# The last gate columns of four SwiGLU layers, moved behind the first seven products of the down projection

## The chip, the cores and the metric

The kernel runs on one core of one Trainium2 chip. The metric is the device time of one execution in microseconds (us). Before the change three runs gave 892.24, 891.83 and 892.64 us, a median of 892.24 us. A separate execution was profiled: 891.0 us, of which 889.1 us are the span from the first to the last instruction. The core's engines are called as in the profile: PE (matrix products; PEld loads their stationary operand), DVE (vector), ACT (scalar), POOL (general purpose) and SP, which here only issues DMA transfers. Each engine works through its own queue in order.

## The reference, cut to what matters

```
def swiglu_ffn(h, w1, w3, w2):
    return (jax.nn.silu(h @ w1) * (h @ w3)) @ w2
...
for i in range(2):
    h = h + 0.5 * swiglu_ffn(rmsnorm(h, ffn_norm1[i]), ffn1_w1[i], ffn1_w3[i], ffn1_w2[i])
    m = rmsnorm(h, mix_norm[i])
    h = h + (conv_module(m, ...) if i == 0 else mla(m, positions, ...))
    h = h + 0.5 * swiglu_ffn(rmsnorm(h, ffn_norm2[i]), ffn2_w1[i], ffn2_w3[i], ffn2_w2[i])
return rmsnorm(h, final_norm)
```

There are 256 rows (tokens) of 1024 channels in float32; the hidden width of an FFN is 2816. So the program is FFN, convolution, FFN, FFN, attention, FFN. The four FFNs are counted as first to fourth here; the change is in all four and nowhere else.

## The kernel before

*Precision.* Each float32 operand x is split into a high part (cast to the fp32r type, on ACT, line 248 or 216) and a low part (x minus the high part, on DVE, line 249 or 202). A product is three matmuls, low weights by high rows, high by high and high by low (`mm3`, lines 332 to 338). The stationary operand is a tile of 128 rows by 128 channels, the moving one 512 columns of a weight block.

*Weight blocks.* Weights come in blocks of 1 MB (`raw`, 128 x 2048 values, four buffers), are split into `hi` and `lo` (five buffers each, in two halves each) and used in the order of the list `blocks`. `load_ahead` keeps a few blocks loaded and cast ahead of the one in use. `n_used` counts the blocks that the products have taken, and `casts[n, i]` is the pair of instructions (ACT, DVE) that splits half `i` of block `n`. All loads are issued by SP.

*One FFN* (`ffn_in`, line 871). Six chunks of hidden columns, c = 0 to 5, the first five of 512 columns and the last of 256. The up products of a chunk fill PSUM banks `u[m, tb]`: m = 0 is the gate side (w1), m = 1 the other (w3), tb = 0 and 1 are the two halves of 128 rows. In the last chunk (`both`) one bank per tb holds both sides. ACT takes Silu of the gate side, DVE multiplies by the other (lines 1005 to 1011); the result `s` is then turned, because the down projection needs hidden columns on the partitions: DVE transposes blocks of 32 x 32 (line 505, `gt`), four DMAs write it to DRAM (line 509, `gd`), one reads it back rearranged (line 514, `gb`), and ACT and DVE split it into `Gh` and `Gl` (line 890, for the last columns 881). That is a `turn`; there is one for each chunk and tb, and one for both halves of the last chunk (`turn_last`). PSUM has eight banks: four under tag A, three under B, one under C.

*The down projection.* `Gh` and `Gl` hold 22 tiles of 128 hidden columns. Blocks 0 to 3 of w2 (tiles 0 to 7) are not multiplied one by one: seven products of sums (a Strassen-like scheme, `seven_products`, line 374) replace eight. Each is 12 matmuls. It forms sums of the weight blocks on DVE (lines 206 to 212) and sums of the rows, whose splits are the `forms`. The first form, of the sum `z22`, is prepared ahead in `down()`; the other three follow in `forms_of` (lines 367 and 370). The four result banks `o` come from tag A, in the order (0,0), (1,0), (1,1), (0,1); the tile `kept` (p5) holds a copy of the second product until two additions have used it. Then the remaining blocks 4 to 10 (tiles 8 to 21) follow, block by block in `Rows.block` (24 matmuls each), the last two or, in the second and third FFN (`apart`), the last three together bank by bank in `Rows.finish`. Tiles 16 to 19 belong to the fifth chunk (blocks 8 and 9), tiles 20 and 21 to the last chunk (block 10). The first bank that `finish` fills in the second and third FFN takes the first row half through blocks 8, 9 and 10, then the second bank does; the second row half comes third and fourth.

*Order.* A scheduler that simulates the program fixes the order of each engine's queue, mostly by the order in which the source emits the instructions and by when they can start in its simulation. `order(ins, first)` adds an edge: `ins` comes behind `first`. Before the change the Silus and products of the last chunk are emitted ahead of the group of seven products, the turn of the fifth chunk's second half too, and only `turn_last` behind it, with its transposition behind the DVE split of the second half of the next block (block 4) and the last four gates' splits behind the first half of block 5.

Of the kernel before, what the change touches and what calls it, by code (L numbers as in the profile page):

```python
# [11 lines left out]
F32 = mybir.dt.float32  # L12
# [7 lines left out]
P = 128  # L20
# [69 lines left out]
def trunk(ctx: ExitStack, tc: tile.TileContext, x, xt, first, pos, invf, gfin, wdw,  # L90
# [14 lines left out]
    def uid(s):  # L105
        n_uid[0] += 1
        return f"{s}_{n_uid[0]}"
# [4 lines left out]
    def bank(tag, name):  # L112
        return ps.tile([P, 512], F32, tag=tag, name=uid(name), bufs=BANKS[tag])
# [244 lines left out]
    def forms_of(sums, sh, sl, late={}):  # L358
        sh, sl = (z.rearrange("p k t -> p (k t)").rearrange("p (n c) -> p n c", c=512) for z in (sh, sl))
        out = {}  # L360
        for i, (n, x) in enumerate(sums):
            if len(x.shape) == 2:
                high, low = (z[:, i].rearrange("p (t i q) -> p t i q", t=4, q=32) for z in (sh, sl))
                x = x.rearrange("p (i t q) -> p t i q", i=4, q=32)
            else:
                high, low = (z[:, i].rearrange("p (k t) -> p k t", t=P) for z in (sh, sl))
            cast = nc.scalar.copy(high, x)
            if n in late:
                late[n] = cast
            nc.vector.tensor_sub(low, x, high.bitcast(F32))  # L370
            out[n] = [z[:, i].rearrange("p (k t) -> p k t", t=P) for z in (sh, sl)]
        return out

    def seven_products(xh, xl, forms, banks, late={}, ahead=False):


        def rows(a, tb):
            k = slice(4 * a, 4 * a + 4)
            return xh[:, k, tbs(tb)], xl[:, k, tbs(tb)]

        def product(a, b, fresh):
            load_ahead(W_BUFS - 1)
            (hi, lo), = weights(1, False)
            for k in range(4):
                c = slice(k * 512, k * 512 + 512)
                before[:] = [mm3(b, a[0][:, k], a[1][:, k], hi[:, c], lo[:, c], fresh and k == 0, k == 3, before, True)]

        n0 = n_used[0]
        before = []
        c11, c21, c12, c22 = banks[0, 0], banks[1, 0], banks[0, 1], banks[1, 1]  # L390
        def copy(to, b, block):
# [12 lines left out]
        product(forms[0], c22, True)  # L404
        kept = tmp.tile([P, 512], F32, tag="s", name=uid("p5"))
        copy(kept, c22, n0 + 5)
        product(forms[1], c21, False)
        add = urgent(nc.vector.tensor_add)(c12, c21, kept)
        if ahead:
            load_to(n0 + 7)  # L410
        for i in range(PIECES if ahead else 1):
            order(casts[n0 + 5, i][1], add.ins)
        if ahead:
            order(casts[n0 + 4, PIECES - 1][1], add.ins)
        for high, low in gates[-2 * NT:-NT] if not late else ():
            order(low, thirds[n0 + 2].ins)
        late_gates = []
        for high, low in gates[-NT:] if not late else ():
            late_gates.append((high, low))
        product(rows(1, 0), c11, False)  # L420
        product(forms[2], c21, False)
        add = urgent(nc.vector.tensor_add)(c22, c21, kept)
        if ahead:
            load_to(n0 + 8)
        for i in range(PIECES if ahead else 1):
            order(casts[n0 + (7 if ahead else 6), i][1], add.ins)
        if ahead:
# [354 lines left out]
    class Rows:  # L782
# [3 lines left out]
                                                      ((0, 0), (0, 1), (1, 0), (1, 1)))}  # L786
            self.seeded = seeded

        def seven(self, forms, late):
            seven_products(self.zh, self.zl, forms, self.o, late)  # L790

        def mm(self, part, i, tb, d, o, f0, f1, o0=0, o1=512, after=(), after_last=()):
            hi, lo = part
# [75 lines left out]
            return ffn_in(act, X, make_next, beside, apart, SEVEN_UP.get(n, ()), n in SEVEN_DOWN)  # L869

    def ffn_in(act, X, make_next, beside, apart, seven_up, seven_down):
        down_sums, first_form = [], {}
        Gh = act.tile([P, NF, S], F32R, tag="Gh", name=uid("Gh"))
        Gl = act.tile([P, NF, S], F32R, tag="Gl", name=uid("Gl"))
        def turn_last(g):

            bv = turn_blocks(act, g, 4, "g", ())
            order(last_turn[0], casts[n_used[0], PIECES - 1][1].ins)
            gh = Gh[:, NF - 2:, :].rearrange("p f (t i q) -> p (f t) i q", i=4, q=32)
            low = Gl[:, NF - 2:, :].rearrange("p f (t i q) -> p (f t) i q", i=4, q=32)  # L880
            gates.append((nc.scalar.copy(gh, bv), nc.vector.tensor_sub(low, bv, gh.bitcast(F32))))

        def turn(c, tb, w, g):

            n = w // P
            f = slice(4 * c, 4 * c + n)
            bv = turn_blocks(act, g[:, :w], n, "g", (), rows4[:, 2 * c + tb, :] if seven_down and c < 2 else None)
            gh = Gh[:, f, tbs(tb)].rearrange("p t (i q) -> p t i q", q=32)
            low = Gl[:, f, tbs(tb)].rearrange("p t (i q) -> p t i q", q=32)
            gates.append((nc.scalar.copy(gh, bv), nc.vector.tensor_sub(low, bv, gh.bitcast(F32))))  # L890
# [37 lines left out]
        for c in range(6):  # L928
# [18 lines left out]
            for m in range(0 if u else 1 if both else 2):  # L947
# [2 lines left out]
                if X.whole and c == 0 and m == 0:  # L950
                    load_to(4)
                for tb in range(NT):
                    u[m, tb] = bank("A", "u")
                steps = [(k, tb) for k in range(KT) for tb in range(NT)]
                if not (X.whole and c == 0 and m == 0):
                    steps.sort(key=lambda t: (t[0] // kn, t[1]))
# [36 lines left out]
                        load_ahead()  # L993
                if c > 0:
                    beside()
            if both:
                last_s = tmp.tile([P, 512], F32, tag="s", name=uid("s"))
            for tb in range(NT):
                if both:
                    s = last_s.rearrange("p (f t c) -> p t f c", t=NT, c=P)[:, tb]  # L1000
                    ug, uu = (u[0, tb][:, v].rearrange("p (f c) -> p f c", c=P) for v in (slice(w), slice(w, 2 * w)))
                else:
                    s = tmp.tile([P, 512], F32, tag="s", name=uid("s"))
                    ug, uu = u[0, tb], u[1, tb]
                silu = nc.scalar.activation(s, ug, AF.Silu, scale=X.r[tb])  # L1005
                if both and seven_down and tb == 0:
                    load_to(n_used[0] + 3)
                    for i in range(PIECES):
                        order(casts[n_used[0] + 2, i][0], silu.ins)
                mul = urgent(nc.vector.tensor_mul) if c in seven_up or c + 1 in seven_up else nc.vector.tensor_mul  # L1010
                mul(s, s, uu)
                if not both:
                    turn(c, tb, w, s)
        o = Rows(Gh, Gl, NF, make_next is Final, seven_down)
        if seven_down:
            both = (xp.tile([P, KT, S], F32R, tag=tag, name=uid("rows")) for tag in ("Xh", "Xl"))
            late = {2: None, 3: None}
            o.seven({**first_form, **forms_of(down_sums[1:], *both, late)}, late)
            turn_last(last_s)
            for gate in gates[-NT - 2:]:  # L1020
                for ins, cast in zip(gate, casts[n_used[0] + 1, 0]):
                    order(ins, cast.ins)
        stage.append("down")
        for i in range(4 if seven_down else 0, NF // 2 - (3 if apart else 2)):
# [879 lines left out]
```

## Time and profile before

| what | value |
| --- | --- |
| median of three runs | 892.24 us |
| profiled execution, total | 891.0 us |
| its span | 889.1 us |
| mean granted clock of the matrix engine | 0.999 |
| DVE 32 x 32 transpositions of gates (L505, 128x512) | 44, median 707 ns |
| DVE gate products (L1011) | 24 of 128x512, 8 of 128x256 |
| down group of the four FFNs, first matmul | 122.3, 388.8, 562.8, 825.7 us |
| turns issued by SP: writes `gd<-gt`, reads `gb<-gd` and `rows<-gd` | 176 of 64 KB, 28 and 16 of 256 KB |

How to read it: a line of the timeline gives start and duration in us, the engine, the line of the kernel, the operation, the tile written and the tiles read, the shape and a count of merged instructions; in brackets stands how long the engine had been idle and what released it. A line of the list of waits gives the engine and operation that waited, what it waited for, the total in us, how often, and the longest. `L` is a line of the kernel. SPq is SP's queue of DMA issues; its duration is that of the issue, not of the transfer. The matrix engine's ends are modelled, so consecutive matmuls overlap in the listing; starts are used for distances.

### The profile page before, as it was taken

How to read it: one execution, taken by the hardware profiler on the slowest of the kernel's cores; microseconds unless marked ns; L12 is line 12 of the kernel's file. 1: busy time of each engine (PE TensorE's matmuls, PEld its weight loads, DVE VectorE, ACT ScalarE, POOL GpSimd, SP SyncE). 2: the span in 40 equal slices, each digit the busy share in tenths (PEclk: the TensorE clock that was granted, in tenths of full speed). 3: DMA queues.
4: the chain of work that ended last, by engine and by line, in shares of the span. 5: the costliest groups of instructions: out<-in, count | busy, mean ns of one | idle time of the engine just before them, and what ended most of it. 6: DMA issues, size and time to landing. Idle time of an engine off the chain costs nothing.

```text
span 889.1 us, 12241 instructions
## 1 busy us (share of the span) xinstructions
PE 881.5 (99%) x4209; PEld 741.9 (83%) x4209; DVE 768.7 (86%) x1106; ACT 580.2 (65%) x1001; POOL 104.8 (12%) x227
## 2 busy tenths in 40 slices
PE   9999999999999999999999999999999999999997
PEld 7888887898988888888888888888899888888886
DVE  6899999789999899989598999995778679999873
ACT  7667858789887656647385465673777666563762
POOL 1000000079952000000010000001400010000000
PEclk9999999999999999999999999999999999999999
DMA  9884929834216945929859278396644558387451
GB/s 336 302 312 148 390 84 354 330 137 148 96 60 230 328 188 204 360 83 358 293 191 335 93 259 308 116 394 200 224 144 142 190 171 334 99 324 257 160 218 48
DMA packets 68174, 198.94 MB, mean 224 GB/s; under 512 B 7952, under 2 KB 38544, under 8 KB 48784
## 3 DMA queue, kind: packets, MB, share of 16 engines
q1 hardware_dynamic: 67680, 197.47, 62.4%
q8 instruction: 33, 0.54, 0.2%
q10 hardware_dynamic: 432, 0.69, 0.2%
q14 instruction: 29, 0.24, 0.1%
HBM read 181.87 MB, written 16.25 MB: 223 GB/s over the span
## 4 chain that ended last, share of the span: by engine, by line
PE 97%; DVE 1%; ACT 0%; DMA 0%; issue 0%; ACTq 0%
PE u L338 17%; PE u L334 17%; PE u L337 17%; PE o L334 9%; PE o L338 9%; PE o L337 9%; PE u L1060 3%; PE gate L1060 3%; PE o L1296 3%; PE u L438 2%; PE sc L1657 1%; PE tp L473 1%; DVE lo L202 1%; PE pairs L1103 1%; PE a L337 1%; PE a L338 1%
## 5 line engine op out<-in xcount | busy, mean ns | idle before, releaser
L249 DVE TENSOR_TENSOR lo<-raw,hi 128x1024 fp32r<-128x1024 f32 (+1 forms) x228 | 267.0, 1212 | 25.8 <-ACT hi L248 25.2
L248 ACT CAST hi<-raw 128x1024 fp32r<-128x1024 f32 (+1 forms) x230 | 229.1, 1044 | 83.9 <-DMA raw<-in_f2w 31.5
L338 PE MATMUL u<-hi,Xl 128*128 128x512 f32 x592 | 230.4, 389 | 0.0
L337 PE MATMUL u<-hi,Xh 128*128 128x512 f32 x592 | 230.3, 389 | 0.0
L334 PE MATMUL u<-lo,Xh 128*128 128x512 f32 x592 | 229.8, 389 | 0.0
L216 ACT CAST hi<-raw 128x1024 fp32r<-128x1024 f32 x112 | 111.5, 1050 | 59.7 <-DVE raw L202 44.8
L202 DVE TENSOR_TENSOR lo<-raw,hi 128x1024 fp32r<-128x1024 f32 x112 | 132.1, 1216 | 2.5 <-ACT hi L216 2.4
L338 PEld LDWEIGHTS u<-hi,Xl 128*128 128x128 f32 x592 | 111.1, 188 | 23.5 <-DVE Xl L492 0.5
L337 PEld LDWEIGHTS u<-hi,Xh 128*128 128x128 f32 x592 | 111.1, 188 | 23.1
L334 PEld LDWEIGHTS u<-lo,Xh 128*128 128x128 f32 x592 | 111.1, 188 | 23.0
L337 PE MATMUL o<-hi,Gh 128*128 128x512 f32 (+1 forms) x276 | 106.5, 386 | 0.0
L338 PE MATMUL o<-hi,Gl 128*128 128x512 f32 (+1 forms) x276 | 106.5, 386 | 0.0
L334 PE MATMUL o<-lo,Gh 128*128 128x512 f32 (+1 forms) x276 | 106.2, 387 | 0.0
L464 POOL TENSOR_TENSOR ms<-ss 128x1 f32<-128x1 f32 x16 | 8.1, 510 | 592.6 <-ACT junk L456 592.6
L202 DVE TENSOR_TENSOR raw<-raw,raw 128x2048 f32<-128x2048 f32 x32 | 73.2, 2288 | 2.4 <-DMA raw<-in_f1w 1.2
L334 PEld LDWEIGHTS o<-lo,Gh 128*128 128x128 f32 x276 | 51.8, 188 | 10.7 <-DVE lo L202 0.2
L337 PEld LDWEIGHTS o<-hi,Gh 128*128 128x128 f32 x276 | 51.8, 188 | 10.4
L338 PEld LDWEIGHTS o<-hi,Gl 128*128 128x128 f32 x276 | 51.8, 188 | 10.4
L1005 ACT ACTIVATE s<-u,R 128x512 f32<-128x512 f32 (+1 forms) x48 | 30.6, 647 | 36.3 <-PE u L338 35.4
L1149 DVE SCALAR_TENSOR_TENSOR acc<-V,dw,acc 128x128 f32<-128x128 f32 (+1 forms) x174 | 53.9, 392 | 0.0
L1170 ACT ACTIVATE prod<-V,dw 128x128 f32<-128x128 f32 (+1 forms) x128 | 45.6, 415 | 1.8 <-POOL Y L1171 1.0
L826 DVE SCALAR_TENSOR_TENSOR h<-o,rh,h 128x512 f32<-128x512 f32 (+1 forms) x18 | 13.0, 720 | 27.2 <-PE o L338 27.2
(271 smaller groups left out, 1303.8 us busy)
## 6 DMA issues: line engine op xcount, KB each, us to landing
raw<-in_f2w SPq DMA_DIRECT2D x66, 1024.0 KB, 6.0
raw<-in_f1w SPq DMA_DIRECT2D x62, 1024.0 KB, 7.0
raw<-in_cw SPq DMA_DIRECT2D x12, 1024.0 KB, 6.2
gd<-gt SPq DMA_DIRECT2D x176, 64.0 KB, 3.8
gb<-gd SPq DMA_DIRECT2D x28, 256.0 KB, 3.3
rows<-gd SPq DMA_DIRECT2D x16, 256.0 KB, 3.0
raw<-in_wo SPq DMA_DIRECT2D x4, 1024.0 KB, 4.8
hd<-rows SPq DMA_DIRECT2D x56, 64.0 KB, 2.3
```

Source lines behind the costliest of these rows:

```text
L202: ins = nc.vector.tensor_sub(out, left, right)
L216: casts[n, i] = nc.scalar.copy(hi[:, c], raw[:, c]), sub(lo[:, c], raw[:, c], hi[:, c].bitcast(F32))
L248: casts[len(loaded), i] = (nc.scalar.copy(hi[:, c], raw[:, c]), low.tensor_sub(lo[:, c], raw[:, c], hi[:, c].bitcast(F32)))
L249: low.tensor_sub(lo[:, c], raw[:, c], hi[:, c].bitcast(F32)))
L334: mm = nc.tensor.matmul(o, ah, bl, start=start, stop=False, skip_group_check=seeded)
L337: nc.tensor.matmul(o, ah, bh, start=False, stop=False, skip_group_check=seeded)
L338: return nc.tensor.matmul(o, al, bh, start=False, stop=stop, skip_group_check=seeded)
L1005: silu = nc.scalar.activation(s, ug, AF.Silu, scale=X.r[tb])
L1060: mm = nc.tensor.matmul(u[:, t], w[:, c], X.x[:, k, t], start=(k == 0), stop=(k == KT - 1))
L1149: dve_last.append(nc.vector.scalar_tensor_tensor(out if j == j1 - 1 else y, v, w, y, op0=ALU.mult, op1=ALU.add))
L1170: prods_last.append(nc.scalar.activation(p, v, AF.Copy, scale=w))
L1296: p = nc.tensor.matmul(o[tb, d], (Zl if kind == "x" else Zh)[:, f, tbs(tb)], (lo if kind == "l" else hi)[:, c], start=(f, kind) == (0, "l" ...
```

## The change

Five things, in all four FFNs:

1. The last chunk's products go to banks of tag B in place of A, so that the four result banks of the group are those of the fifth chunk.
2. The Silus and products of the last chunk are emitted behind the group of seven products, each behind the split (ACT or DVE) of the second half of block 5.
3. The turn of the fifth chunk's second half (c = 4, tb = 1) is emitted behind the group too (`late_turns`), its transposition behind the DVE split of the second half of block 4. `turn_last` has no edge of its own any more.
4. The copy `kept` goes into the place of the sum z22 (`down_sums[0][1]`), whose split has been made, in place of a temporary tile, since both temporary tiles stay in use longer.
5. The splits of the last four gates: the first two stay behind the first half of block 5, the third goes behind the first half of block 6, the last behind the second half of block 6. The edge that held a weight cast behind the last chunk's first Silu is gone.

```diff
-    def seven_products(xh, xl, forms, banks, late={}, ahead=False):
+    def seven_products(xh, xl, forms, banks, late={}, ahead=False, kept=None):
...
-        kept = tmp.tile([P, 512], F32, tag="s", name=uid("p5"))
+        if kept is None:
+            kept = tmp.tile([P, 512], F32, tag="s", name=uid("p5"))
...
             bv = turn_blocks(act, g, 4, "g", ())
-            order(last_turn[0], casts[n_used[0], PIECES - 1][1].ins)
...
-                    u[m, tb] = bank("A", "u")
+                    u[m, tb] = bank("B" if both else "A", "u")
...
-            if both:
-                last_s = tmp.tile([P, 512], F32, tag="s", name=uid("s"))
-            for tb in range(NT):
-                if both:
-                    s = last_s.rearrange("p (f t c) -> p t f c", t=NT, c=P)[:, tb]
-                    ug, uu = (u[0, tb][:, v].rearrange("p (f c) -> p f c", c=P) for v in (slice(w), slice(w, 2 * w)))
+            for tb in range(0 if both else NT):
+                s = tmp.tile([P, 512], F32, tag="s", name=uid("s"))
+                nc.scalar.activation(s, u[0, tb], AF.Silu, scale=X.r[tb])
+                mul = urgent(nc.vector.tensor_mul) if c in seven_up or c + 1 in seven_up else nc.vector.tensor_mul
+                mul(s, s, u[1, tb])
+                if 2 * c + tb < 9:
+                    turn(c, tb, w, s)
                 else:
...
-                silu = nc.scalar.activation(s, ug, AF.Silu, scale=X.r[tb])
-                if both and seven_down and tb == 0:
-                    load_to(n_used[0] + 3)
-                    for i in range(PIECES):
-                        order(casts[n_used[0] + 2, i][0], silu.ins)
...
+                    late_turns.append((c, tb, w, s))
...
-            o.seven({**first_form, **forms_of(down_sums[1:], *both, late)}, late)
+            o.seven({**first_form, **forms_of(down_sums[1:], *both, late)}, late, down_sums[0][1])
+
+            for t in late_turns:
+                turn(*t)
+                order(last_turn[0], casts[n_used[0], PIECES - 1][1].ins)
+            last_s = tmp.tile([P, 512], F32, tag="s", name=uid("s"))
+            for tb in range(NT):
+                s = last_s.rearrange("p (f t c) -> p t f c", t=NT, c=P)[:, tb]
+                ug, uu = (u[0, tb][:, v].rearrange("p (f c) -> p f c", c=P) for v in (slice(w), slice(w, 2 * w)))
+                silu = nc.scalar.activation(s, ug, AF.Silu, scale=X.r[tb])
+                mul = nc.vector.tensor_mul(s, s, uu)
+                for ins, cast in zip((silu, mul), casts[n_used[0] + 1, PIECES - 1]):
+                    order(ins, cast.ins)
             turn_last(last_s)
-            for gate in gates[-NT - 2:]:
-                for ins, cast in zip(gate, casts[n_used[0] + 1, 0]):
+            for gate, behind_, i in zip(gates[-4:], (1, 1, 2, 2), (0, 0, 0, PIECES - 1)):
+                for ins, cast in zip(gate, casts[n_used[0] + behind_, i]):
                     order(ins, cast.ins)
```

More of the change, by code (lines that the diff above doesn't have):

```diff
@@ L787, in __init__, with seven @@
             self.seeded = seeded
-        def seven(self, forms, late):
-            seven_products(self.zh, self.zl, forms, self.o, late)
+        def seven(self, forms, late, kept):
+            seven_products(self.zh, self.zl, forms, self.o, late, kept=kept)
         def mm(self, part, i, tb, d, o, f0, f1, o0=0, o1=512, after=(), after_last=()):
@@ L871, in ffn_in @@
     def ffn_in(act, X, make_next, beside, apart, seven_up, seven_down):
-        down_sums, first_form = [], {}
+        down_sums, first_form, late_turns = [], {}, []
         Gh = act.tile([P, NF, S], F32R, tag="Gh", name=uid("Gh"))
@@ L995, in ffn_in @@
                     beside()
-            if both:
-                last_s = tmp.tile([P, 512], F32, tag="s", name=uid("s"))
-            for tb in range(NT):
-                if both:
-                    s = last_s.rearrange("p (f t c) -> p t f c", t=NT, c=P)[:, tb]
-                    ug, uu = (u[0, tb][:, v].rearrange("p (f c) -> p f c", c=P) for v in (slice(w), slice(w, 2 * w)))
-                else:
-                    s = tmp.tile([P, 512], F32, tag="s", name=uid("s"))
-                    ug, uu = u[0, tb], u[1, tb]
-                silu = nc.scalar.activation(s, ug, AF.Silu, scale=X.r[tb])
-                if both and seven_down and tb == 0:
-                    load_to(n_used[0] + 3)
-                    for i in range(PIECES):
-                        order(casts[n_used[0] + 2, i][0], silu.ins)
[L1010 to L1013, printed above, removed]
+            for tb in range(0 if both else NT):
[5 more added lines that the diff above has]
+                    turn(c, tb, w, s)
+                else:
+                    late_turns.append((c, tb, w, s))
         o = Rows(Gh, Gl, NF, make_next is Final, seven_down)
```

## The prediction

> **What bounds the kernel now.** First the page, for which engine the end hangs on.
>
> ```profile
> span 889.1 us, 12241 instructions
> PE 881.5 (99%) x4209; PEld 741.9 (83%) x4209; DVE 768.7 (86%) x1106; ACT 580.2 (65%) x1001; POOL 104.8 (12%) x227
> PE 97%; DVE 1%; ACT 0%; DMA 0%; issue 0%; ACTq 0%
> ```
>
> The matmul engine is busy for 99% of the span and 97% of the chain that ended last is its own work. The change takes no matmul away and adds none. So it can gain only what the matmul engine still waits, and it can lose wherever the shifted work comes too late. The second view is therefore the list of what the matmul engine waited for.
>
> ```profile
> PE warm L326 <- DVE still L321: 1.0, 1, 1.0
> PE o L334 <- DVE lo L202: 0.4, 1, 0.4
> PE u L438 <- ACT Xh L667: 0.2, 1, 0.2
> ```
>
> The first and third row are at the start of the program. Only the second, 0.4 us once, lies in a place that the change touches: a down product (o) waits for the low half of a weight block. The ends of matmuls are modelled, so I look at starts, in the timeline of the matmul engine in the first FFN.
>
> ```profile
> 135.64 0.39 PE L338 MATMUL o<-hi,rows 128*128 128x512 f32 x1
> 136.40 0.47 PE L334 MATMUL o<-lo,rows 128*128 128x512 f32 x1 [0.37 <-DVE lo L202]
> 136.70 0.40 PE L337 MATMUL o<-hi,rows 128*128 128x512 f32 x1
> ```
>
> The regular distance comes from the same view in the second FFN, where the last three blocks begin:
>
> ```profile
> 429.56 0.39 PE L334 MATMUL o<-lo,Gh 128*128 128x512 f32 x1
> ...
> 432.28 0.39 PE L334 MATMUL o<-lo,Gh 128*128 128x512 f32 x1
> 432.51 0.39 PE L337 MATMUL o<-hi,Gh 128*128 128x512 f32 x1
> 432.74 0.39 PE L338 MATMUL o<-hi,Gl 128*128 128x512 f32 x1
> ```
>
> From 429.56 to 432.28 there are 12 matmuls, so the regular distance is 2.72/12 = 0.227 us. In the first FFN the steps are 0.76 and 0.30 us: 0.53 + 0.07 = 0.60 us lost, in the sixth product of the down group. The other three down groups have no row among the waits: nothing is lost there, and nothing is to be won.
>
> Third, why the sixth product waited: the vector engine and then the scalar engine before that time.
>
> ```profile
> 117.24 0.71 DVE L505 STREAM_TRANSPOSE gt<-s 128x512 f32<-128x512 f32 x1
> 117.86 2.32 DVE L202 TENSOR_TENSOR lo<-raw,hi 128x1024 fp32r<-128x1024 f32 x2
> 120.25 0.42 DVE L1011 TENSOR_TENSOR s<-s,u 128x256 f32<-128x256 f32 x1
> ...
> 123.50 0.41 DVE L1011 TENSOR_TENSOR s<-s,u 128x256 f32<-128x256 f32 x1
> 124.20 4.63 DVE L202 TENSOR_TENSOR lo<-raw,hi 128x1024 fp32r<-128x1024 f32 x4 [0.29 <-ACT hi L216]
> ...
> 135.03 2.36 DVE L202 TENSOR_TENSOR lo<-raw,hi 128x1024 fp32r<-128x1024 f32 x2
> ```
>
> ```profile
> 122.24 0.62 ACT L367 CAST rows<-rows 128x512 fp32r<-128x512 f32 x1 [2.02 <-PE u L337]
> 122.76 0.47 ACT L1005 ACTIVATE s<-u,R 128x256 f32<-128x256 f32 x1
> 123.13 3.89 ACT L216 CAST hi<-raw 128x1024 fp32r<-128x1024 f32 x4
> ```
>
> The low half that was late is the first of the pair at 135.03. The vector engine ran up to it from 117 with one gap of 0.29 us, so it was simply full. Three instructions in that stretch are ones that the change moves behind the group: the transposition of the fifth chunk's second half (117.24) and the two gate products of the last columns (120.25, 123.50). The Silu at 122.76 stands ahead of the weight casts at 123.13.
>
> **The change part by part.**
> *Taken out ahead of the late half.* On the vector engine: one transposition and two products. Neighbouring starts overlap by about 0.08 us (117.24 + 0.71 = 117.95, next at 117.86), so they hold the engine for 0.62 + 0.34 + 0.33 = 1.3 us. On the scalar engine the Silu holds 122.76 to 123.13 = 0.37 us. What the late half gains lies between 0.37 us (if the cast pair at 123.13 still starts only after the row cast, which waits for the matmul engine until 122.24) and 1.3 us (if the vector engine's fullness is all that counts). The stall is 0.60 us. I take the upper end, since the engine was full throughout and the weight casts do not depend on the row cast: the stall goes. **Gain 0.6 us**; at the lower bound it would be 0.4 us.
>
> *Banks.* The last columns' products get banks of group B, and so their Silus no longer stand before the second product of the group. No row shows the matmul engine waiting for a bank there, so this alone is worth 0. What it allows is the later Silu. The sum z22 now holds p5: it was read by its cast long before, and no instruction is added. Cost 0.
>
> *Added behind the group.* The same transposition with its four writes and one read through DRAM, two Silus, two products, in every FFN. The matmul engine does not wait for them at once: the fifth chunk's gates are needed in block 8, the last columns' gates in block 10. I take the second FFN, where three blocks are finished together and the need is earliest: the vector engine,
>
> ```profile
> 407.71 0.71 DVE L505 STREAM_TRANSPOSE gt<-s 128x512 f32<-128x512 f32 x1
> 408.34 1.18 DVE L249 TENSOR_TENSOR lo<-raw,hi 128x1024 fp32r<-128x1024 f32 x1
> 409.44 1.89 DVE L890 TENSOR_TENSOR Gl<-gb,Gh 128x512 fp32r<-128x512 f32 x3
> 411.25 8.03 DVE L249 TENSOR_TENSOR lo<-raw,hi 128x1024 fp32r<-128x1024 f32 x7
> ...
> 425.02 0.68 DVE L881 TENSOR_TENSOR Gl<-gb,Gh 128x512 fp32r<-128x512 f32 x1
> ```
>
> and the issues of the sync queue:
>
> ```profile
> 385.40 1.90 SPq L509 DMA_DIRECT2D gd<-gt  x4
> 388.68 0.34 SPq L514 DMA_DIRECT2D gb<-gd  x1
> ...
> 408.44 1.93 SPq L509 DMA_DIRECT2D gd<-gt  x4
> ...
> 415.79 0.33 SPq L514 DMA_DIRECT2D gb<-gd  x1
> ```
>
> Before, the last columns are transposed at 407.71, behind block 4's low half; their low gate ends at 425.02 + 0.68 = 425.70, 18.0 us later. Block 10 reads the high gate at 432.28 and the low one at 432.74, so there are 7.0 us to spare. After, the fifth chunk's transposition takes the place at 407.71. The last columns' Silus wait for block 5's second high half, their products for its second low half. That half starts at 411.25 now, and 0.60 us earlier without the third gate at 409.44: it ends near 411.8. Two products (0.34 each) lead to a transposition at 412.5, **4.8 us later** than now. If the scheduler lets block 6's two low halves pass (2 x 1.15 us by the row of seven), it is **7.1 us later**. I take the middle, 5.9, since no row prefers one end. The fifth chunk's own gate then comes where the last columns' gate came, 425.7; its second rows are used in block 8 only after two banks of 18 matmuls, at 429.56 + 36 x 0.227 = 437.7: covered by 12 us.
>
> What the sync queue is moved past: five issues more per FFN behind the group, between loads of later weight blocks. The DMA engines are full there:
>
> ```profile
> 380.00:392.00 12.00, 12.00 (x55) 9.94 (x54) 10.11 (x11) 5.47 (x8) 0.00 (x0) 1.00 0.34 89
> 403.00:431.00 28.00, 28.00 (x125) 23.17 (x125) 24.11 (x25) 19.56 (x23) 0.00 (x0) 1.00 1.01 396
> 431.00:434.00 3.00, 3.00 (x15) 2.49 (x14) 2.30 (x3) 0.77 (x1) 0.00 (x0) 1.00 0.67 259
> ```
>
> (The columns behind the engines are granted clock, DMA share and GB/s.) From 380 to 392 only two turns move, 0.34 x 12 / 2 = 2.05 us of all DMA engines for each. So the moved turn puts 0 to 2.05 us of delay on the last gate, which comes out at 425.70 + 4.8 = 430.5 at the earliest and 425.70 + 7.1 + 2.05 = 434.9 at the latest, against 432.74. With the middle shift and no extra queueing, since the 18.0 us were already measured in full queues, it is 431.6, **hidden with 1.1 us to spare**. I cost it at 0; without that cover it is 2.1 us. The third FFN has the same pattern. In the first and fourth only two blocks are finished together, so the gate is needed a block (24 x 0.227 = 5.4 us) later: covered at both ends.
>
> [...] The rows: write to read took 388.68 - 385.40 = 3.3 us on quiet DMA engines and 415.79 - 408.44 = 7.35 us on full ones. [...]
>
> **Sum.** The profiled execution took 891.0 us (span 889.1 and 1.9 around it); 891.0 - 0.6 = 890.4. The median of the runs shown is 892.24, 1.24 above that execution, so the same step gives **891.6 us**.
>
> **The rivals.**
> *1. Slower: the last gate comes too late in the second and third FFN.* This is the one mechanism that can cost more than the stall is worth. For it speaks that the latest end above (434.9) is 2.1 us past the need, and that two engines take work in order:
>
> ```profile
> 429.76 2.01 ACT L248 CAST hi<-raw 128x1024 fp32r<-128x1024 f32 x2 [2.97 <-PE o L338]
> ```
>
> ```profile
> 430.85 2.36 DVE L249 TENSOR_TENSOR lo<-raw,hi 128x1024 fp32r<-128x1024 f32 x2 [2.62 <-ACT hi L248]
> ```
>
> If the gate is queued behind these pairs, its low half starts at 433.1 and ends at 433.8, 1.1 us late even with no further delay. Both add up at most to about 2.1 + 1.1 = 3.2 us in each of two FFNs, 6.4 us. It decides from an end at 432.74 on; beyond 432.74 + 1.2 it shows in the total as slower. With the latest end without queueing behind the pairs, twice 2.1 us: 891.6 + 4.2 = **895.8 us**. Against it: 3 us of gap before each pair, into which a gate at 431 or sooner nearly fits.
> *2. It does nothing that shows.* The sixth product's half is late for another reason: the subtraction ahead of it or the row casts set its time, and the freed 1.3 us turn into gaps. **892.2 us**. For it speaks the 2.02 us that the scalar engine waited for the matmul engine at 122.24; against it the vector engine without gaps.
> *3. The handover to the next layer.* The moved DMA work (2.05 us) pushes the weight loads ahead of the first row writes of the next FFN.
>
> ```profile
> 445.88 0.39 PE L334 MATMUL u<-lo,Xh 128*128 128x512 f32 x1
> ```
>
> ```profile
> 444.09 1.28 ACT L625 ACTIVATE Xh<-rows,G 128x128 fp32r<-128x128 f32 x4 [0.45 <-DMA rows<-hd]
> ```
>
> The first row cast ends about 0.4 us after 444.09 and is used at 445.88, 1.4 us of cover; the idle third of the DMA engines from 431 to 434 takes 1.0 us. With that, nothing is lost; without it 0.65 us in each of two handovers, **892.9 us**.
> *4. Much faster.* This would need a loss on the matmul engine that the starts do not show; about **889 us**, from nothing in the trace.
>
> **How the numbers follow.** Forecast 0.40; rival 1 0.31, of which 0.04 is too small to count; rival 2 0.19; rival 3 0.07; rival 4 0.03. About 0.2%, 1.8 us, is what a measurement of this kernel can tell from no change. Faster by more than that: 0.03. Slower: 0.27. Within: 0.40 + 0.19 + 0.07 + 0.04 = 0.70. The likeliest case alone spans 891.2 to 892.0; the range has to take in most of rival 1, so **890.9 to 895.8 us**.
>
> **What would show it.** Right: in the first FFN the starts around 135 to 137 are 0.227 us apart and no product waits for DVE L202; the two short products (L1011, 128x256) stand behind the group in all four FFNs; the last gate (L881) ends before 432 in the second FFN. Wrong: a row in the waits of the matmul engine with Gh or Gl as what it waited for, at block 10 of the second and third FFN (rival 1), or with Xh or Xl at the start of the next layer (rival 3). If the wait for DVE L202 stays, the term of 0.6 us was wrong (rival 2).

## The result, and the profile after

The changed kernel took 904.71 us (median of four runs, 903.58 to 906.18) against 892.04 us for the kernel before (891.07 to 892.64): a ratio of 1.0147, interval 1.0135 to 1.0159. It is 12.7 us slower, and above the predicted range. The profiled execution of the changed kernel was the slowest of the four, 906.18 us with a span of 904.3; its mean granted clock was 0.991 and that of the other three 0.996, so of the four it shows the cost of the clock at its largest.

First the page and the list of what the matrix engine waited for, of the changed kernel.

```profile
span 904.3 us, 12246 instructions
PE 888.8 (98%) x4209; PEld 746.3 (83%) x4209; DVE 768.3 (85%) x1106; ACT 578.9 (64%) x1001; POOL 102.8 (11%) x227
```

```profile
PE u L334 <- ACT Xh L626: 4.6, 1, 4.6
PE a L334 <- ACT Xh L626: 3.5, 1, 3.5
PE warm L326 <- DVE still L321: 1.0, 1, 1.0
PE u L334 <- DVE lo L249: 0.3, 1, 0.3
```

No row names Gh or Gl. The two new waits are for `Xh`, the normed rows of the layer that follows the second FFN (`u`) and the third (`a`, attention). The matrix engine is also busy for 7.3 us more with the same 4209 matmuls, which a wait cannot explain. The timeline of the matrix engine shows both, at the end of the second FFN:

```profile
446.99 0.39 PE L338 MATMUL o<-hi,Gl 128*128 128x512 f32 x1
451.97 0.80 PE L334 MATMUL u<-lo,Xh 128*128 128x512 f32 x1 [4.59 <-ACT Xh L626]
452.56 0.63 PE L337 MATMUL u<-hi,Xh 128*128 128x512 f32 x1
452.99 0.63 PE L338 MATMUL u<-hi,Xl 128*128 128x512 f32 x1
...
456.40 0.63 PE L337 MATMUL u<-hi,Xh 128*128 128x512 f32 x1
456.83 0.53 PE L338 MATMUL u<-hi,Xl 128*128 128x512 f32 x1
457.20 0.39 PE L334 MATMUL u<-lo,Xh 128*128 128x512 f32 x1
457.43 0.40 PE L337 MATMUL u<-hi,Xh 128*128 128x512 f32 x1
```

The step over the wait is 4.98 us in place of 0.227: 4.75 lost. Then matmuls start 0.43 us apart until 457.20. From 446.99 to 457.20 there are 14 steps: 10.21 - 14 x 0.227 = 7.0 us lost, so 2.3 us of it behind the wait. The view by windows (engines PE, PEld, DVE, ACT, POOL, then granted clock, DMA share, GB/s) shows what goes with the wide steps, after both FFNs:

```profile
452.00:457.00 5.00, 5.00 (x12) 3.94 (x13) 3.17 (x9) 5.00 (x11) 0.00 (x0) 0.50 0.38 112
457.00:462.00 5.00, 5.00 (x24) 4.12 (x23) 5.00 (x9) 4.04 (x10) 0.00 (x0) 0.99 0.62 206
...
632.00:638.00 6.00, 5.75 (x14) 4.54 (x15) 4.57 (x11) 5.93 (x16) 1.07 (x4) 0.50 0.42 102
```

The granted clock is 0.50 over 5 and 6 us behind the two waits. At the third FFN the matrix engine's timeline has

```profile
628.35 0.39 PE L338 MATMUL o<-hi,Gl 128*128 128x512 f32 x1
632.25 0.80 PE L334 MATMUL a<-lo,Xh 128*128 128x512 f32 x1 [3.51 <-ACT Xh L626]
...
638.23 0.39 PE L338 MATMUL a<-hi,Xl 128*128 128x512 f32 x1
```

and 16 steps from the first to the last of these rows: 9.88 - 16 x 0.227 = 6.2 us, of which 3.90 - 0.23 = 3.7 are the wait. Together 13.2 of the 15.2 us by which this profiled execution is longer (906.18 - 891.0).

Why `Xh` is late is seen on the vector engine. Before, the first finished bank was added to `h` at 433.91, the next ones 4 us apart:

```profile
433.91 0.75 DVE L826 SCALAR_TENSOR_TENSOR h<-o,rh,h 128x512 f32<-128x512 f32 x1 [0.70 <-PE o L338]
434.70 0.71 DVE L505 STREAM_TRANSPOSE rows<-h 128x512 f32<-128x512 f32 x1
437.93 0.75 DVE L826 SCALAR_TENSOR_TENSOR h<-o,rh,h 128x512 f32<-128x512 f32 x1 [2.52 <-PE o L338]
```

After:

```profile
409.04 0.70 DVE L506 STREAM_TRANSPOSE gt<-s 128x512 f32<-128x512 f32 x1
...
411.97 1.22 DVE L249 TENSOR_TENSOR lo<-raw,hi 128x1024 fp32r<-128x1024 f32 x1
413.11 0.75 DVE L1019 TENSOR_TENSOR s<-s,u 128x256 f32<-128x256 f32 x2
413.77 3.49 DVE L249 TENSOR_TENSOR lo<-raw,hi 128x1024 fp32r<-128x1024 f32 x3
417.18 0.71 DVE L506 STREAM_TRANSPOSE gt<-s 128x512 f32<-128x512 f32 x1
...
432.18 2.36 DVE L249 TENSOR_TENSOR lo<-raw,hi 128x1024 fp32r<-128x1024 f32 x2 [1.96 <-ACT hi L248]
434.46 0.69 DVE L881 TENSOR_TENSOR Gl<-gb,Gh 128x512 fp32r<-128x512 f32 x1
440.68 0.75 DVE L827 SCALAR_TENSOR_TENSOR h<-o,rh,h 128x512 f32<-128x512 f32 x1 [5.54 <-PE o L338]
441.47 0.71 DVE L506 STREAM_TRANSPOSE rows<-h 128x512 f32<-128x512 f32 x1
442.11 0.71 DVE L827 SCALAR_TENSOR_TENSOR h<-o,rh,h 128x512 f32<-128x512 f32 x1
```

The first transposition in this fence stands in the place of before's at 407.71, so this execution runs 1.33 us later here anyway. The first addition is 6.77 us later, 5.44 net, and the second only 1.4 us behind it. That is not a late input of a matmul, since the matrix engine worked without a gap all the while (busy for 40.00 us of the 40 from 407 to 447); it worked in another order. Of the 72 matmuls that finish the four banks (three blocks of 24, in the queue of the matrix engine), the last one of each bank was:

| kernel | 1st bank | 2nd | 3rd | 4th |
| --- | --- | --- | --- | --- |
| before | 18 | 36 | 54 | 72 |
| after | 42 | 46 | 54 | 72 |

The first bank ends 24 matmuls later: 24 x 0.227 = 5.45 us, the 5.44 of the addition. The lines of the source that emit these matmuls are unchanged. The scheduler drew up this order: the low gate of the last columns ends at 434.46 + 0.69 = 435.15, in place of 425.70, and the products of blocks 8 and 9 for other banks stand ahead of the first bank's block 10.

### The profile page after: what moved, and what is told of

It is laid out like the page before. It is cut to its first block, busy times and chain, and to the rows that moved or that the text cites. A ratio compares the mean times of both kernels' runs of the same rounds, so it can differ in the third digit from the quotient of the medians.

```text
span 904.3 us, 12246 instructions
## 1 busy us (share of the span) xinstructions
PE 888.8 (98%) x4209; PEld 746.3 (83%) x4209; DVE 768.3 (85%) x1106; ACT 578.9 (64%) x1001; POOL 102.8 (11%) x227
## 4 chain that ended last, share of the span: by engine, by line
PE 95%; DMA 2%; DVE 1%; SPq 1%; issue 0%; ACT 0%; DVEq 0%; ACTq 0%
PE u L334 16%; PE u L338 16%; PE u L337 16%; PE o L334 9%; PE o L337 9%; PE o L338 9%; PE u L1063 3%; PE gate L1063 3%; PE u L439 2%; PE o L1299 2%; PE sc L1660 1%; PE tp L474 1%; PE a L334 1%; PE pairs L1106 1%; PE a L337 1%; PE a L338 1%
## 5 line engine op out<-in xcount | busy, mean ns | idle before, releaser
L249 DVE TENSOR_TENSOR lo<-raw,hi 128x1024 fp32r<-128x1024 f32 (+1 forms) x228 | 267.3, 1210 | 25.1 <-ACT hi L248 24.6
L457 ACT ACTIVATE junk<-h 128x512 f32<-128x512 f32 x24 | 15.0, 629 | 28.7 <-DVE h L827 26.0
```

The costliest lines, as they stand in the source:

```text
L249: low.tensor_sub(lo[:, c], raw[:, c], hi[:, c].bitcast(F32)))
```

## The experiments

The theory (O, order): the last gate comes later in the scheduler's simulation, so it moves matmuls that don't need it ahead of block 10; two banks then end together and late, the chain from the addition of the first row half to `Xh` starts late, the matrix engine waits, and its clock halves. Rival Q: the moved turn's DMA issues and traffic delay the rows of the next layer. Rival B: there is simply too much work of the vector engine behind the group, and any order of it would cost this.

**The two halves of the change apart.** In the first kernel the fifth chunk's turn keeps its old place; in the second only that turn moves, while the last columns' Silus and products stay ahead of the group (the banks, the place of `kept` and the places of the gates' splits are as in the changed kernel in both).

```diff
-                if 2 * c + tb < 9:
+                if True:
```

> The changed kernel, but the fifth chunk's second turn stands where it stood before; only the Silus, products and turn of the last columns are late. Theory O: the first finishing bank ends after 25 of 72 matmuls in place of 42 (before: 18), 7 x 0.227 = 1.6 us later than before against 1.4 us of cover: 0.2 us lost at each of two handovers and no drop of the clock, 892 to 893.5 us. Rival Q: 2.05 us of transfers per FFN are back ahead of the group, 891.5 to 893 us; this run tells the two apart only together with the one that leaves the turn late.

```diff
+            if both:
+                last_s = tmp.tile([P, 512], F32, tag="s", name=uid("s"))
+                for tb in range(NT):
...
+                    nc.scalar.activation(s, ug, AF.Silu, scale=X.r[tb])
+                    nc.vector.tensor_mul(s, s, uu)
...
```

> The changed kernel, but the Silus and products of the last columns stand where they stood before; only the fifth chunk's second turn is moved behind the group. Theory O (the last gate comes late in the scheduler's simulation, so it puts the matmuls of the finishing banks in another order, the first bank ends late and the handover to the next layer with it): the order of the finishing banks is back to 18, 36, 54 and 72 of 72 matmuls, no wait at the handover, 891.0 to 892.5 us. Rival Q (the moved turn's transfers crowd the queue and the DMA engines ahead of the handover): nothing of that turn is undone here, so 902 to 906 us.

Measured (the kernel before, run beside all these kernels, took 891.71 to 891.94 us): 892.09 us, ratio 0.9996 (0.9987 to 1.0006), banks ending at 25, 36, 54, 72; and 891.85 us, 0.9997 (0.9988 to 1.0006), banks at 18, 36, 54, 72. Neither half costs anything alone. In the second the turn's five DMA issues are behind the group as in the changed kernel, and nothing is lost: this speaks against Q. In the first the last columns' transposition and low gate fall between those of the kernels before and after:

```profile
414.82 0.71 DVE L506 STREAM_TRANSPOSE gt<-s 128x512 f32<-128x512 f32 x1
...
430.27 0.69 DVE L881 TENSOR_TENSOR Gl<-gb,Gh 128x512 fp32r<-128x512 f32 x1 [0.65 <-ACT Gh L881]
...
435.60 0.75 DVE L827 SCALAR_TENSOR_TENSOR h<-o,rh,h 128x512 f32<-128x512 f32 x1 [2.00 <-PE o L338]
```

The low gate ends at 430.96, and the first bank at 25. In the second kernel its row is

```profile
427.95 0.68 DVE L881 TENSOR_TENSOR Gl<-gb,Gh 128x512 fp32r<-128x512 f32 x1
```

So with low gates that end at 425.70 (before) and 428.63 the order stays, at 430.96 the first bank gives way by 7 matmuls, at 435.15 (after) by 24. The executions are shifted against each other by up to 1.3 us, which does not change this: the first of the 72 matmuls starts at 429.56, 430.08, 429.66 and 430.89, and counted from there the low gate ends 3.86 us ahead, 1.45 ahead, 1.30 behind and 4.26 behind.

**The order alone, both ways.** The changed kernel with the finishing banks held one behind the other, and the kernel before with these matmuls forced into the late order:

```diff
+                        if apart and i:
+                            after = (*after, done)
```

> The changed kernel with one edge more: in the second and third FFN each finishing bank's matmuls come behind the last matmul of the bank before, as they ran before the change. Theory O: the last gate is still late (its low half ended 1.5 us past the need), so the matrix engine waits for the gate in block 10, 1 to 2 us in each of two FFNs, and the handover's wait of 4 to 5 us and the slow clock behind it go: 893.5 to 897 us. Rival Q: the wait at the handover stays, 902 to 906 us.

```diff
+            if apart:
+                A, B, C, E = (0, 1), (0, 0), (1, 0), (1, 1)
+                steps = [*((A, a, j) for a in (0, 1) for j in (0, 1)), *((B, a, j) for a in (0, 1) for j in (0, 1)),
+                         (C, 0, 0), (C, 0, 1), (A, 2, 0), (B, 2, 0), (C, 1, 0), (A, 2, 1), (B, 2, 1), (C, 1, 1),
+                         (C, 2, 0), (C, 2, 1), *((E, a, j) for a in (0, 1, 2) for j in (0, 1))]
+                for (tb, d), a, j in steps:
...
+                    done = mm3(self.o[tb, d], ..., () if done is None else (done,), self.seeded)
```

> The kernel before, with nothing of the change, but with the finishing matmuls of the second and third FFN forced into the order that the changed kernel has: the first two banks end after 42 and 45 of 72 matmuls. Theory O: this order alone makes the loss, a wait of 4 to 5 us at each of two handovers and a lower clock behind each, 902 to 906 us. Rival Q: the turns and their transfers are where they were, so 891.5 to 893 us.

With before's order forced on the change: 894.49 us, ratio 1.003 (1.002 to 1.004), banks ending at 18, 36, 54, 72. With the late order forced on the kernel before, nothing else changed: 903.94 us (901.53 to 905.45), ratio 1.0125 (1.0101 to 1.0148), banks ending at 42, 45, 54, 72. So the order makes the loss with no turn, Silu or gate moved, and Q and B have nothing left to explain. The waits of the latter kernel, and its first additions:

```profile
PE u L334 <- ACT Xh L625: 4.9, 1, 4.9
PE a L334 <- ACT Xh L625: 3.1, 1, 3.1
```

```profile
439.97 1.41 DVE L826 SCALAR_TENSOR_TENSOR h<-o,rh,h 128x512 f32<-128x512 f32 x2 [6.14 <-PE o L338]
```

The former shows what the late gate costs where the order stays, in the waits and in the timeline:

```profile
PE o L338 <- DVE Gl L883: 1.6, 2, 0.8
```

```profile
433.24 0.40 PE L337 MATMUL o<-hi,Gh 128*128 128x512 f32 x1
434.43 0.50 PE L338 MATMUL o<-hi,Gl 128*128 128x512 f32 x1 [0.80 <-DVE Gl L883]
```

A step of 1.19 us, 0.96 lost, once in each of the two FFNs, and not much more: 2.6 us in the total. This is the stall that rival 1 of the prediction had priced, at 2.1 us each. The scheduler avoided it and paid five times as much at the handover.

**How much of it is the clock.** The changed kernel with 38 and 30 matmuls of a constant tile into an unused bank, placed behind the last down product of the second and third FFN. They compute nothing that is used.

```diff
+                        if i == 3:
+                            keep_warm(38 if n_ffns[0] == 2 else 30, "C", done)
```

> The changed kernel, and at the end of the second and third FFN 38 and 30 small matmuls into an unused bank, on operands that are there, which fill some 4.6 and 3.6 us of the waits of 5.0 and 3.9 us. Theory C (the slow matmuls behind each wait, 0.427 us apart in place of 0.227, come from the idle time before): the wait stays, the slow stretches go, 2 to 2.6 us each: 899 to 901.5 us. Rival: the slow stretches come from something else in the next layer's start: 903 to 906 us.

Measured: 900.67 us (900.0 to 901.0), ratio 1.0093 (1.0079 to 1.0106). Rows of its timeline and its windows:

```profile
446.68 4.32 PE L326 MATMUL warm<-still 128*128 128x256 bf16 x38
451.25 0.50 PE L334 MATMUL u<-lo,Xh 128*128 128x512 f32 x1 [0.24 <-ACT Xh L626]
451.59 0.40 PE L337 MATMUL u<-hi,Xh 128*128 128x512 f32 x1
451.82 0.40 PE L338 MATMUL u<-hi,Xl 128*128 128x512 f32 x1
```

```profile
452.00:457.00 5.00, 4.97 (x22) 3.75 (x22) 3.16 (x8) 5.00 (x10) 0.00 (x0) 1.00 0.39 107
```

The same 5 us now hold 22 matmuls and not 12, at a granted clock of 1.00 and not 0.50, with the start nearly as late as before: 4.80 us behind the last down product (446.45), where it was 4.98. So some 4 us of the 12.7 (904.71 - 900.67 = 4.0, from runs made at different times) are the halved clock behind the two waits, and the other 8.7 or so the waits themselves.

**How late a bank may end.** The kernel before with the first bank forced to end after 30 of the 72, and the changed kernel with block 6's low halves held behind the last columns' transposition:

```diff
...
+                steps = [*((A, a, j) for a in (0, 1) for j in (0, 1)), *((B, a, j) for a in (0, 1) for j in (0, 1)),
+                         (A, 2, 0), (A, 2, 1), (B, 2, 0), (B, 2, 1),
+                         *((q, a, j) for q in (C, E) for a in (0, 1, 2) for j in (0, 1))]
...
```

> The kernel before, with the finishing matmuls of the second and third FFN forced so that the first bank ends after 30 of 72 matmuls (before: 18) and the others after 36, 54 and 72 as before. Theory O with its price, (matmuls late) x 0.227 us less 1.4 us of cover: 12 x 0.227 - 1.4 = 1.3 us of wait at each of two handovers, no slow stretch behind a wait that short, 893.5 to 895.5 us. Rival: the handover hangs on the second bank too, so that the first alone costs nothing, 891 to 892.5 us.

```diff
             turn_last(last_s)
+            for i in range(PIECES):
+                order(casts[n_used[0] + 2, i][1], last_turn[0].ins)
```

> The changed kernel with one edge more: the last columns' transposition comes ahead of block 6's low halves on the vector engine (it stood behind these two and one more). The first finishing bank then ends after 27 of 72 matmuls. Theory O: 9 x 0.227 - 1.4 = 0.6 us at each of two handovers, 892 to 894 us. Rival: the wait does not grow with the number of matmuls but comes at once, 896 us or more.

Measured: 893.94 us, ratio 1.0021 (1.0012 to 1.0031), with banks at 30, 36, 54, 72 and waits of 0.3 and 0.8 us for `Xh`; and 891.42 us, ratio 0.9998 (0.9988 to 1.0007), with banks at 27, 36, 54, 72 and no wait for `Xh` at all. The first lay in the range expected of it, the second under it: nine matmuls, 2.0 us, cost nothing, though the cover was thought to be 1.4. The first uses the same rewritten loop as the kernel with the late order, so the rewriting as such does not make that kernel's 12 us.

The cover is not one number, since the read back hangs on more than the first bank. In the profile before, SP's queue has the row writes of both first banks ahead of the read back of the second FFN:

```profile
435.44 5.77 SPq L509 DMA_DIRECT2D hd<-rows  x8
441.37 1.54 SPq L514 DMA_DIRECT2D rows<-hd  x2
```

The first four of the eight are issued by 437.27, the other four from 439.45 on, when the second bank is there. So the first bank alone could come some 2 us later in the second FFN and the read back would not move: with the edge it is issued at 442.27, 11.97 us behind the first of the 72 matmuls, and 11.81 us behind it before. This is the rival of the first of these two runs, that the handover hangs on the second bank too, and it holds in part. In the third FFN only four writes stood ahead of the read back before (609.52 and 613.26), and the cover was 3.4 us (`Xh` at 616.14, used at 619.96); with the edge eight stand there, which may have used up part of it (not tried by itself). In the first half of the change alone, a bank that ends seven matmuls late meets a wait of 0.4 us: there the rows take 3.8 us from the issue of the read back to `Xh` (442.25 to 446.07), against 2.7 with the edge (442.27 to 445.01). What makes this read longer was not tried.

**The change in other arrangements.** The last columns' Silus and products already behind block 5's first half, with the low halves of block 5's second half and of block 6 behind their transposition:

```diff
-                for ins, cast in zip((silu, mul), casts[n_used[0] + 1, PIECES - 1]):
+                for ins, cast in zip((silu, mul), casts[n_used[0] + 1, 0]):
...
+            for i in range(PIECES):
+                order(casts[n_used[0] + 2, i][1], last_turn[0].ins)
+            order(casts[n_used[0] + 1, PIECES - 1][1], last_turn[0].ins)
```

> The changed kernel with everything still behind the group, but the last columns sooner: their Silus and products come behind block 5's first half (not its second), and their transposition comes ahead of the low half of block 5's second half and of block 6 on the vector engine. Theory O: it is only the time of that transposition that the order of the finishing banks hangs on; the banks end after 18, 36, 54 and 72 matmuls again, no handover is late, 891.0 to 892.5 us. Rival B (having both moved parts behind the group is too much work there, whatever its order): still above 897 us.

Then the last columns turned first, behind block 4, and the fifth chunk's second half behind block 5; all four gates' splits go behind block 5's first half, as before the change:

```diff
...
-                for ins, cast in zip((silu, mul), casts[n_used[0] + 1, PIECES - 1]):
+                for ins, cast in zip((silu, mul), casts[n_used[0], PIECES - 1]):
...
-            for gate, behind_, i in zip(gates[-4:], (1, 1, 2, 2), (0, 0, 0, PIECES - 1)):
+            order(last_turn[0], casts[n_used[0], PIECES - 1][1].ins)
+            for t in late_turns:
+                turn(*t)
+                order(last_turn[0], casts[n_used[0] + 1, PIECES - 1][1].ins)
+            for gate, behind_, i in zip(gates[-4:], (1, 1, 1, 1), (0, 0, 0, 0)):
```

> The changed kernel with the two moved parts swapped: behind the group the last columns' Silus, products and turn come first (behind block 4), the fifth chunk's second turn after it (behind block 5). Theory O: the last gate is in time, banks end after 18, 36, 54 and 72, 891.0 to 892.5 us. Rival B: above 897 us.

Last, the change in the first and fourth FFN only, by an `apart` in each of its conditions:

```diff
-                    u[m, tb] = bank("B" if both else "A", "u")
+                    u[m, tb] = bank("B" if both and not apart else "A", "u")
...
```

> The change in the first and fourth FFN only; the second and third as before. Theory O: nothing is lost at the handovers; the first FFN's down group loses 0.3 us in place of 0.7: 891.0 to 892.0 us, which the measurement can hardly tell from the kernel before. Rival: the change costs something in every FFN, then 2 to 6 us above before.

Measured: 892.03 us, ratio 1.0002 (0.9993 to 1.0011); 892.89 us, 1.0011 (1.0002 to 1.0019); and 892.56 us, 1.0008 (0.9993 to 1.0023). The first lies in its range, the second 0.4 and the third 0.6 us above theirs. In the second a small loss is left: its list of waits has 0.7 us for the low rows `Xl` behind the second FFN. In all three the banks end at 18, 36, 54, 72. Everything that the change puts behind the group is still there in the first two, and 12 us are gone, against B. The first turns the last columns at 413.60, the second at 411.27. No arrangement is faster than the kernel before by more than its interval, so there is no better version to show.

## Why the prediction was wrong, step by step

*What bounds the kernel.* Right: the matrix engine, and the change could only lose where shifted work comes too late. The list of waits shows the place.

*The gain of 0.6 us in the first FFN.* Mis-sized. The steps around the sixth product are now 0.30 and 0.34 us, in place of 0.76 and 0.30:

```profile
137.11 0.39 PE L338 MATMUL o<-hi,rows 128*128 128x512 f32 x1
137.41 0.50 PE L334 MATMUL o<-lo,rows 128*128 128x512 f32 x1
137.75 0.40 PE L337 MATMUL o<-hi,rows 128*128 128x512 f32 x1
```

That is 0.42 us gained in this profile, the prediction's lower bound; a gain in the time itself no run shows. The 1.3 us freed on the vector engine became a gap, as rival 2 had it:

```profile
124.36 0.69 DVE L370 TENSOR_TENSOR rows<-rows,rows 128x512 fp32r<-128x512 f32 x1 [1.32 <-ACT rows L367]
```

The row cast that it waits for (ACT, 123.71) waits itself for the matrix engine. The 2.02 us of that wait in the profile before were the sign, and I weighed the full vector engine above it.

*Banks and the copy `kept`, cost 0.* Nothing in the trace speaks against it; no wait for a bank appeared.

*The last gate's shift, 4.8 to 7.1 us, 5.9 taken.* Too small. From 407.71 to 417.18 are 9.47 us, less 1.33 by which this execution runs later: 8.1. Between the two products and the transposition stand not at most two low halves but three (413.77, x3). The low gate ends at 435.15; less the 1.33 us that is 433.8, inside the bound of 434.9 and 1.1 us past the need at 432.74. From the transposition to that end it takes 18.0 us as before, so nothing of the 0 to 2.05 us for the fuller queue appeared. What stood last in the gate's way was its place in the queues: the low half follows directly on the pair of weight splits at 432.18, and less the 1.33 us it runs from 433.1 to 433.8, which is what rival 1 had given for a gate queued behind these pairs.

One reading under this step does not hold. The 7.35 us from write to read that the prediction sets beside full DMA engines contain more than the write: between the write (408.44) and its read back SP's queue has two weight loads, issued from 412.49 to 415.11, and the read back follows at 415.79.

*"Hidden", cost 0.* This is the step that failed, and not by its size. It measured the gate against the place of block 10 in the order of before, and took that order to stay; rival 1, priced at 895.8 us, took the same. Where the order is made to stay, block 10 waits as rival 1 had it, for 0.96 us in each FFN, and the time is 894.49. But the order is drawn up anew, from simulated times that no trace shows. The scheduler's answer to a late gate was to finish the first two banks 24 and 10 matmuls later, which kept the matrix engine busy and moved the loss 13 us down the line, from block 10 to the next layer's start, where it became 12.7 us in place of 2.6.

*The handover.* Rival 3 had the right place and the cover of 1.4 us, but its push was the DMA work, which cost nothing here (where the turn alone moves, the ratio is 0.9997). What arrived there was the 5.45 us of the order. From the first addition to `Xh` it takes 444.09 - 433.91 = 10.18 us before and 10.84 after:

```profile
451.52 1.28 ACT L626 ACTIVATE Xh<-rows,G 128x128 fp32r<-128x128 f32 x4 [2.27 <-DMA rows<-hd]
```

The loss at the wait should then be 5.45 + 0.66 - 1.4 = 4.71 us; it is 4.75. In the third FFN the cover was larger, 3.4 us, and the stretch grew more, from 616.14 - 607.99 = 8.15 to 631.80 - 622.05 = 9.75: 5.45 + 1.60 - 3.4 = 3.65 us, and 3.67 were lost at the wait. The stretch may be longer because ten row writes now stand ahead of the read back, in place of eight and four; that was not tried by itself.

```profile
442.21 6.39 SPq L510 DMA_DIRECT2D hd<-rows  x10
448.70 0.90 SPq L515 DMA_DIRECT2D rows<-hd  x2
```

*The sum.* Where no handover is late, the change costs nothing, but the forecast gain does not show either: with the edge at block 6 it took 891.42 us beside 891.71 for the kernel before, and turned sooner 892.03 beside 891.94, both inside their intervals. The rest of the 15.2 us of the profiled execution lies ahead of the change: the down matmul at 135.64 starts at 137.11, 1.47 us later. The engines' instruction orders up to 115 us are identical in both kernels (the 0.3 us for `lo` L249 in the waits lies there, at 90 us), and 0.9 of the 1.47 us are there after the first 7 us, so this is put down to the execution, not to the change.

Left open: why the scheduler put three low halves ahead of the last transposition, and from which simulated time on it changes the order of the banks. The runs only bracket the latter, by the end of the low gate on the chip, counted from the first of the 72 matmuls: at 1.4 us ahead of it (also in the kernel turned sooner, 430.35 and 431.74) the order stays, at 0.5 us behind it (the edge at block 6, 430.80 and 430.30) it has begun to give way, though the matrix engine needs the gate only 3.2 us behind that first matmul. The gate's time on the chip does not settle the order alone: the first bank ends at 27 there, and at 25 in the kernel whose gate comes 1.30 us behind.

## What to carry to other kernels

Where a scheduler draws up the queues, a late operand need not show as a wait at its reader: other work is moved ahead, and what shifts is the end of the results that were to be finished first. So ask of a moved input not only whether its reader can wait, but which result's last matmul could be moved behind others, and what starts from that result; compare the place of each bank's last matmul in the queue before reading any wait. An order that matters to the next layer is worth an explicit edge, and here the change with an edge on the competing vector work (block 6's halves) cost nothing, while with one on the matmuls alone it cost 2.6 us.

## What the runs showed of the hardware

The two waits of the matrix engine cost half and two thirds more than they lasted (7.0 us for 4.75, 6.2 for 3.7). Behind gaps of 4.6 and 3.5 us the granted clock was 0.50 (behind 4.9 and 3.1 us in the kernel before with the late order forced on it 0.53 from 452 to 457 and 0.54 from 632 to 638), and matmuls with 512 columns started 0.427 us apart in place of 0.227, for 5.2 us after the first gap (451.97 to 457.20) and 6.0 after the second (632.25 to 638.23). The windows of the changed kernel bound the first stretch of half clock:

```profile
450.29:457.11 6.82, 5.14 (x12) 4.08 (x13) 3.33 (x9) 5.59 (x12) 0.38 (x2) 0.50 0.52 168
```

Behind a gap of 0.8 us (a step of 1.2), in the changed kernel with the banks held in order, the clock stayed at 1.00:

```profile
434.00:439.00 5.00, 4.57 (x20) 3.78 (x21) 1.84 (x3) 0.00 (x0) 0.00 (x0) 1.00 0.87 309
```

The clock was 0.50 for 6.8 us each time, from 450.29 to 457.11 and from 631.19 to 638.02, and 0.99 to 1.00 just ahead of these stretches and behind them. It fell while the matrix engine still waited, 2.9 and 2.5 us behind the modelled ends of the last matmuls (447.38 and 628.74). With matmuls without use in the gaps the clock was 1.00 in them and behind them (447.0 to 451.9, 452 to 457, 628.4 to 638.2), and the time some 4 us shorter (900.67 for 904.71). How long a gap must be for this, no run shows: the clock stayed at 1.00 behind the one of 0.8 us and fell 2.9 and 2.5 us into two longer ones. Nor was the cost the same in every execution: the four of the kernel before with the late order forced on it had mean clocks of 0.991, 0.991, 0.993 and 0.997, and took 905.45, 904.61, 903.28 and 901.53 us.
